# Two-operand GpSimd work of the mixers moved to VectorE, ScalarE and TensorE in five places, and the ranges of a group norm taken one by one

## The chip, the cores and the metric

One core of a Trainium2 chip runs the whole kernel. The metric is the device time of one execution in microseconds (us), the median of three runs. The engines are TensorE (PE in the profile, its weight loads PEld), VectorE (DVE), ScalarE (ACT), GpSimd (POOL) and SyncE (SP), which issues most transfers.

## The reference, cut to what matters

One decoder layer over 512 tokens and 16 meta tokens, width 1024, in float32: a mixer with two kinds of heads, then a mixture of experts.

```python
xn = _rmsnorm(h, norm_mix_w)                      # h: 528 x 1024
r, k, v, qm, km, vm, om, gm = split(xn @ w_in)
y_a = _rwkv7_time_mix(xn, r, k, v, ...)           # 8 heads of 64
y_b = _mlstm_mix(qm, km, vm, om, gm, ...)         # 4 heads, chunks of 64 in the reference
h = h + concatenate([y_a, y_b]) @ w_out
h = h + _hmoe(_rmsnorm(h, norm_ffn_w), ...)       # top group of 4, then 2 of its 8 experts
return _rmsnorm(h, norm_final_w)[:, 16:]

# in _rwkv7_time_mix
a = sigmoid(a0 + (xa @ a_la) @ a_lb)
kk = normalized(k * k_k);  k = k * (1 + (a - 1) * k_a)
S = S * decay + (S @ -kk) * (kk * a) + v * k      # a step for each token
y = group_norm(S @ r) * lnx_w + lnx_b
y = (y + sum(r * k * r_k) * v) * g
```

## The kernel before, in words

The tokens lie along the columns of tiles of 128 channels x 528 tokens. The recurrence is computed in chunks of 64 tokens (and one of the 16 meta tokens), which takes the inverse of a unit triangular matrix for each chunk and head.

**Head (lines 546 to 701).** The eight blocks of the input arrive as tiles xT[k]. For each, ScalarE makes the scaled high part and VectorE the low part (`xl`, a scalar-tensor-tensor), and TensorE multiplies them with the first two blocks of the input projection. `squares` (L613) squares each block, on ScalarE for even k and on VectorE for odd k, and GpSimd adds each square to `acc` (L620). Then two ones-matmuls with `acc` (L695) and Ln and Exp give `rstd`. `lora_mix` and `lora_split` (L647, L656) on VectorE and ScalarE prepare the LoRA block, the first projection of the planned part.

**The planned part (from L642 to `W.run()`).** The mixers are generators, each with a rank (`W.add`). A planner, `Weave` (L355), runs the one of lowest rank that is ready. What "ready" means is told by `Clock` (L181), a written table of costs for each engine; GpSimd's tensor_tensor has a rate of its own there, twice VectorE's. The order in which generators issue instructions is the program's order for TensorE and SyncE, which are under a manual schedule; the other engines' instructions are ordered by the tile scheduler.

- `projections` (L1008): the blocks of the input projection in the order of `PLAN`, each 48 matmuls (24 for "o"). `prepare` (L671) makes the high part of the next block on ScalarE, and its low part, 128x1024, on `lo_by`: GpSimd once mark "P3" is set (the products of all four head pairs are done), VectorE before that, and VectorE again when the recurrence is over, but for kind "q".
- `decays`, `norms`, `heads`, `products` (L778 to 957): for each of four pairs of heads j, the decay, the normalized key and the blocks MV, Bbd and Kbd that the products on TensorE read. In `heads` (L836) GpSimd does the diagonal of MV, nk times alpha, kp times kx, two of the four copies into E, and r times r_k times kp, in two instructions.
- `inverse0` and `inverse` (L1357, L1372): `interleaved` (L1335) inverts by column steps of two dependent tensor_tensor instructions, a product and an addition; the 16-row inverse runs on GpSimd, the 32-row one on VectorE. Matmuls on 32x32 blocks finish the latter.
- `chain` (L1476): the recurrence over nine chunks. At its end it takes the tiles `Gw` and `sq` and sets the mark "chain".
- `variances`, `variance`, `outputs_a`, `gated` (L1545 to 1584): the group norm of each of four ranges of 128 tokens (Square, a matmul, Ln), one Exp over all four ranges, and then for each range the product with the gate (on GpSimd), two VectorE instructions and the split into high and low parts, `ya`.
- `states` (L1191), `gates`, `scores`, `outputs_b`: the mLSTM heads. `mixer`: the output projection, the residual, the router. `prefetch` fetches expert weights as soon as there is room.

Memory is handed out by `Space` and `Arena`: `A.get` takes a tile at once or fails, `W.room` lets the generator wait until there is room.

**Experts (from L2053).** Sixteen pairs of experts, twelve weight blocks of 1 MiB each. A block is fetched when a buffer is free.

Of the kernel before, what the change touches and what calls it, by code (L numbers as in the profile page):

```python
# [17 lines left out]
L = 528  # L18
# [417 lines left out]
def layer(ctx, tc, a, out, dbg=None, stop=None):  # L436
# [145 lines left out]
    acc = A.get([128, L], name="acc")  # L582
# [29 lines left out]
    A.put(idle_)  # L612
    def squares(k):  # L613
        sq = A.get([128, L], name="sq") if k else acc
        if k % 2:
            V.tensor_tensor(sq, xT[:, k], xT[:, k], op=OP.mult)
        else:
            S.activation(sq, xT[:, k], AF.Square)
        if k:
            G.tensor_tensor(acc, acc, sq, op=OP.add)  # L620
            A.put(sq)

    first_block(0, 2)
    for k in range(8):
        S.activation(xh[k], xT[:, k], AF.Copy, scale=c("nmw", k))
        V.scalar_tensor_tensor(xl[k], xT[:, k], c("nmw", k), xh[k].bitcast(F32), op0=OP.mult, op1=OP.subtract)
        proj_k(pk, kh_, kl_, k)
        if not k:
            first_block(2, 8)
            A.put(kraw)  # L630
        if k == 2:
            k1h, k1l, kput1 = split_block(stream.loaded.pop(0), hi_by=S, lo_by=V)
            for i in range(k):
                proj_k(pk1, k1h, k1l, i)
        if k >= 2:
            proj_k(pk1, k1h, k1l, k)
            squares(k - 2)
    for k in range(6, 8):
        squares(k)

# [30 lines left out]
    def prepare(kind):  # L671

        lo_by = V if late() and kind != "q" or "P3" not in W.marks else G
# [19 lines left out]
    pss = B.get(2, "pss", rest)  # L693
    for h in range(2):
        P.matmul(pss[:, h, :264], m("ones"), acc[:, 264 * h:264 * h + 264], start=True, stop=True)  # L695
# [4 lines left out]
    A.put(xT, acc)  # L700
# [135 lines left out]
    def heads():  # L836

        for j in range(4):
# [5 lines left out]
            G.tensor_tensor(MV[:, :, 128:192], i64[:, None].to_broadcast([128, 8, 64]),  # L844
                            DT[:, j, 1:9][:, :, None].to_broadcast([128, 8, 64]), op=OP.mult)
            G.tensor_scalar(mv0[:, NM:], i64, DT[:, j, 0:1], 0.0, op0=OP.mult, op1=OP.add)
            G.tensor_tensor(nk, nk, al, op=OP.mult)
            kp = al
            S.activation(kp, al, AF.Identity, scale=c("k_a", j), bias=dv[:, 12 + j:13 + j])
            G.tensor_tensor(kp, kp, kx[j], op=OP.mult)  # L850
# [13 lines left out]
            for p in range(2):  # L864
                for i in range(2):
                    (S.copy if p else gcopy)(E[i][PAR[p], :, j, p], MV[PAR[p], 4 * i:4 * i + 4, 0:128])
            G.tensor_scalar(r[:, NM:], r[:, NM:], c("r_k", j), 0.0, op0=OP.mult, op1=OP.add)
            G.tensor_tensor(r[:, NM:], r[:, NM:], kp[:, NM:], op=OP.mult)
# [322 lines left out]
    def states():  # L1191
# [3 lines left out]
        for tb in range(-1, 3):  # L1195
# [6 lines left out]
            kw = A.get([128, 4, 64], name="kw")  # L1202
# [154 lines left out]
    def inverse0():  # L1357
# [8 lines left out]
        yield from interleaved(G, XL0, lambda s: NL0[:, s + 1:, s], NM, tm0, 99)  # L1366
# [5 lines left out]
    def inverse():  # L1372
# [39 lines left out]
        A.put(NL, XL, Y1, Y2, *tmps, *Zs)  # L1412
        dump("X", Bt)
# [62 lines left out]
    def chain():  # L1476
# [40 lines left out]
        Gw = A.get([128, 4, T], name="Gw")  # L1517
        sqs.append(A.get([128, 4, 4, 128], name="sq"))
        B.put(pU, pY)
        every.extend(rest)  # L1520
# [24 lines left out]
    def variances():  # L1545

        f = "p j x -> p (j x)"
        yield from until("chain")
        for tb in range(4):
            W.add(1, variance(tb, yT[tb].rearrange(f), sqs[0][:, tb].rearrange(f)))  # L1550
        yield from until(*(f"var{tb}" for tb in range(4)))
        S.activation(sqs[0], sqs[0], AF.Exp, scale=-0.5)
        W.mark("var")
# [13 lines left out]
    def outputs_a():  # L1567
        yield from until("var", "Gw")
        for tb in range(4):
            ya[tb] = yield from W.room(A, 2, [128, 4, 128], F32R, "ya", (ar_s[tb],))  # L1570
            gated(tb, sqs[0][:, tb])
            W.mark(f"ya{tb}")
            yield
        A.put(sqs[0], BV, Gw)

    def gated(tb, sq):
        y = yT[tb]
        G.tensor_tensor(y, y, Gw[:, :, 128 * tb:128 * tb + 128], op=OP.mult)
# [748 lines left out]
```

## Time and profile before

| | |
|---|---|
| median of 3 runs | 916.93 us (914.76 to 918.5) |
| the profiled execution | 914.68 us |
| its span, first to last instruction | 912.8 us |
| PE busy | 841.9 us (92%) |
| DVE busy | 434.1 us (48%) |
| ACT busy | 270.8 us (30%) |
| POOL busy | 224.0 us (25%) |
| mean granted TensorE clock | 0.96 |

The span is what the profile shows; the time of the execution has some two microseconds around it. Most instructions of the mixers carry the line L304, that of a helper that records every operation, so they are told apart by engine, operation, tile and shape: arF is the arena of most tiles, arS and arR those of high and low parts, arW that of the output weights, accs the accumulators of TensorE. A busy PE is one with a matmul in flight, and the clock is the share of full speed that was granted to it. What a stage's busy time means depends on what it waits for, so the rows below are taken by stage.

### The profile page before, as it was taken

What the parts mean: (1) busy time and instruction counts of PE and PEld (TensorE: products, weight loads), DVE (VectorE), ACT (ScalarE), POOL (GpSimd) and SP (SyncE); (2) the same over time, 40 slices, a digit from 0 to 9 for tenths busy, and PEclk for the clock granted to TensorE, in tenths of its full rate; (3) what the DMA queues carried; (4) which work ended last, traced back from release to release, by engine and by line L of the source; (5) the groups of instructions that cost most, each with busy time, mean ns of one, the idle gap of its engine ahead of it and who ended that gap; (6) DMA issues with size and microseconds to landing.
All of it is one profiled execution on the core that took longest, in us unless ns stands there. A gap on an engine that the chain in (4) does not pass through costs nothing.

```text
span 912.8 us, 13508 instructions
## 1 busy us (share of the span) xinstructions
PE 841.9 (92%) x5385; PEld 517.7 (57%) x5386; DVE 434.1 (48%) x821; ACT 270.8 (30%) x522; POOL 224.0 (25%) x297
## 2 busy tenths in 40 slices
PE   7969989879999997998999999999999999989994
PEld 5868878769999776887343444433344323323331
DVE  7677766995444668328132333423333223313324
ACT  5756655324435773333100110101110011001102
POOL 6064553553545156254000000000000000000002
PEclk9989999986998999998999999999999999999998
DMA  6200113201100137928999999999999999999992
GB/s 236 70 24 24 47 70 83 65 27 55 47 25 25 48 107 291 405 78 332 394 419 421 420 421 419 421 420 420 421 418 420 422 421 421 420 420 422 420 379 96
DMA packets 45141, 239.50 MB, mean 262 GB/s; under 512 B 8944, under 2 KB 9328, under 8 KB 21008
## 3 DMA queue, kind: packets, MB, share of 16 engines
q1 hardware_dynamic: 42192, 228.56, 62.5%
q0 software_dynamic: 2160, 7.87, 2.2%
q10 hardware_dynamic: 720, 2.15, 0.6%
q8 instruction: 44, 0.72, 0.3%
q14 instruction: 25, 0.20, 0.1%
HBM read 234.36 MB, written 4.19 MB: 261 GB/s over the span
## 4 chain that ended last, share of the span: by engine, by line
PE 55%; DMA 20%; DVE 15%; ACT 5%; issue 3%; POOL 2%; SPq 0%; ACTq 0%; DVEq 0%; POOLq 0%
PE accs L304 22%; PE accs L2067 17%; DVE arF L304 10%; PE accs L2112 7%; DMA arF<-wgu 7%; ACT arF L304 3%; PE accs L1990 3%; DMA arH<-wgu 2%; DMA arF<-wdn 2%; DMA arN<-wdn 2%; DMA arN<-wgu 2%; DMA arM<-wgu 2%; PE accs L1991 2%; DMA arF<-wo 1%; POOL arF L304 1%
## 5 line engine op out<-in xcount | busy, mean ns | idle before, releaser
L304 PE MATMUL accs<-arS,arR 128*128 128x264 f32 (+2 forms) x1136 | 182.6, 312 | 10.6 <-DVE arR L304 5.0
L304 PEld LDWEIGHTS accs<-arS,arR 128*128 128x128 f32 (+1 forms) x1136 | 160.4, 198 | 23.1 <-DVE arR L304 5.4
L304 PE MATMUL accs<-arF 64*64 64x64 f32 (+18 forms) x1223 | 129.7, 271 | 29.1 <-DVE arF L304 15.6
L1993 DVE TENSOR_TENSOR arF<-arF,accs 128x512 f32<-128x512 f32 x124 | 80.8, 684 | 102.5 <-PE accs L1991 101.0
L304 PEld LDWEIGHTS accs<-arF 128*128 128x128 f32 (+7 forms) x1202 | 103.5, 159 | 41.3 <-DVE arF L304 11.6
L2067 PE MATMUL accs<-arF 128*64 128x512 f32 x488 | 115.8, 605 | 5.9 <-DMA arF<-wgu 5.9
L1803 POOL DMA_INDIRECT arM<-hd,arF x15 | 14.3, 956 | 380.0 <-DVE arF L1794 368.6
L304 POOL TENSOR_TENSOR arF<-arF 128x528 f32<-128x528 f32 (+13 forms) x101 | 90.7, 901 | 65.9 <-DVE arF L304 44.0
L304 DVE TENSOR_TENSOR arF<-arF 64x16 f32<-64x16 f32 (+33 forms) x183 | 90.5, 541 | 6.5 <-POOL arF L304 4.2
L2089 ACT ACTIVATE arF<-accs,arF 128x512 f32<-128x512 f32 x16 | 11.0, 687 | 252.4 <-PE accs L2067 252.4
L2067 PEld LDWEIGHTS accs<-arF 128*64 128x64 f32 x488 | 32.3, 138 | 76.0 <-issue 57.4
L304 ACT ACTIVATE arF<-arF 128x528 f32<-128x528 f32 (+8 forms) x108 | 57.9, 559 | 49.6 <-DVE arF L304 34.1
L2122 DVE SCALAR_TENSOR_TENSOR arO<-accs,arF,arO 128x1024 fp32r<-128x1024 f32 x15 | 19.3, 1284 | 103.8 <-ACT arO L2121 103.8
L304 POOL TENSOR_SCALAR arF<-arF 64x256 f32<-64x256 f32 (+9 forms) x97 | 55.4, 573 | 44.0 <-ACT arF L304 19.3
L2112 PE MATMUL accs<-arF 128*64 128x512 f32 x280 | 62.5, 595 | 0.5 <-issue 0.5
L304 ACT COPY arF<-accs 64x256 f32<-64x256 f32 (+6 forms) x119 | 43.2, 370 | 65.4 <-PE accs L304 31.2
L1990 PE MATMUL accs<-arO,OHT 128*128 128x512 f32 x124 | 57.4, 463 | 0.0
L304 DVE TENSOR_TENSOR arF<-accs,arF 128x528 f32<-128x528 f32 (+7 forms) x81 | 35.5, 462 | 34.5 <-PE accs L304 20.8
L2067 PE MATMUL accs<-arN,arF 128*64 128x512 f32 x200 | 47.5, 600 | 2.6 <-DMA arN<-wgu 2.5
L1991 PE MATMUL accs<-arO,OHT 128*128 128x512 f32 x124 | 48.9, 394 | 0.0
L2067 PE MATMUL accs<-arM,arF 128*64 128x512 f32 x200 | 46.9, 600 | 1.7 <-DMA arM<-wgu 1.7
L304 PE MATMUL accs<-arW,arS 128*128 128x512 f32 x192 | 47.7, 406 | 0.0
(140 smaller groups left out, 924.2 us busy)
## 6 DMA issues: line engine op xcount, KB each, us to landing
arF<-wgu SPq DMA_DIRECT2D x61, 1024.0 KB, 19.8
arF<-wdn SPq DMA_DIRECT2D x35, 1024.0 KB, 20.4
arN<-wgu SPq DMA_DIRECT2D x25, 1024.0 KB, 19.8
arM<-wgu SPq DMA_DIRECT2D x25, 1024.0 KB, 19.8
arH<-wgu SPq DMA_DIRECT2D x16, 1024.0 KB, 20.9
arN<-wdn SPq DMA_DIRECT2D x15, 1024.0 KB, 21.1
arF<-wb SPq DMA_DIRECT2D x23, 512.0 KB, 3.6
arH<-wdn SPq DMA_DIRECT2D x5, 1024.0 KB, 20.0
```

The lines of the kernel that those rows point to most:

```text
L304: r = f(*args, **kw)
L1803: nc.gpsimd.indirect_dma_start(out=xt[p % 2], out_offset=None, in_=hd, in_offset=bass.IndirectOffsetOnAxis(ap=idx[:, p % 2:p % 2 + 1], axi ...
L1990: P.matmul(pq, lhs, oh[:, hs], start=True, stop=False)
L1991: P.matmul(pq, lhs, ol[:, hs], start=False, stop=True)
L1993: V.tensor_tensor(hv, hv, pq, op=OP.add)
L2067: P.matmul(pgu[64 * e:64 * e + 64, h], x[:, k, 64 * e:64 * e + 64], w[:, D * e + 512 * h:D * e + 512 * h + 512], start=(k == 0), stop=(k = ...
L2089: S.activation(av, pgu[:, 0], AF.Silu, scale=r1_)
L2112: P.matmul(pdn[64 * e:64 * e + 64, h], aT[:, k, 64 * e:64 * e + 64], w[:, D * h + 512 * e:D * h + 512 * e + 512], start=(k == 0), stop=(k ...
L2122: V.scalar_tensor_tensor(ol, pdf, g1_, oh.bitcast(F32), op0=OP.mult, op1=OP.subtract)
```

## The change

Seven edits:

1. `squares`: every block is squared on ScalarE; VectorE adds the squares in pairs (odd k), and the ones-matmuls sum the four pairs in PSUM (`summed`), two of them inside the head's loop, two where the sum was formed before. `acc` and its seven GpSimd additions go.
2. `prepare`: the low parts stay on VectorE until a new mark, "inverse", which `inverse` sets at its end, instead of "P3".
3. `heads`: the diagonal of MV, nk times alpha and kp times kx go to VectorE; all four copies into E are ScalarE's; r times r_k times kp is one scalar-tensor-tensor on VectorE.
4. `inverse0`: the 16-row inverse's steps run on VectorE.
5. `chain`, `variances`: `sq` is four tiles of 128x512 instead of one of 128x2048, with an Exp for each; `Gw` and these tiles are taken with `W.room`.
6. `gated`: the product with the gate goes to VectorE.
7. `states`: `kw` is taken with `W.room`.

```diff
+    pss = B.get(2, "pss", rest)
+    sqs2 = []
+
     def squares(k):
-        sq = A.get([128, L], name="sq") if k else acc
+        sqs2.append(A.get([128, L], name="sq"))
+        S.activation(sqs2[k], xT[:, k], AF.Square)
         if k % 2:
-            V.tensor_tensor(sq, xT[:, k], xT[:, k], op=OP.mult)
-        else:
-            S.activation(sq, xT[:, k], AF.Square)
-        if k:
-            G.tensor_tensor(acc, acc, sq, op=OP.add)
-            A.put(sq)
+            V.tensor_tensor(sqs2[k], sqs2[k], sqs2[k - 1], op=OP.add)
+
+    def summed(k):
+
+        for h in range(2):
+            P.matmul(pss[:, h, :264], m("ones"), sqs2[k][:, 264 * h:264 * h + 264], start=(k == 1), stop=(k == 7))
...
         if k >= 2:
             proj_k(pk1, k1h, k1l, k)
-            squares(k - 2)
-    for k in range(6, 8):
         squares(k)
+        if k == 5:
+            summed(1)
+        if k == 7:
+            summed(3)
...
-        lo_by = V if late() and kind != "q" or "P3" not in W.marks else G
+        lo_by = V if late() and kind != "q" or "inverse" not in W.marks else G
...
-    pss = B.get(2, "pss", rest)
-    for h in range(2):
-        P.matmul(pss[:, h, :264], m("ones"), acc[:, 264 * h:264 * h + 264], start=True, stop=True)
+    summed(5)
+    summed(7)
...
-            G.tensor_tensor(MV[:, :, 128:192], i64[:, None].to_broadcast([128, 8, 64]),
+            V.tensor_tensor(MV[:, :, 128:192], i64[:, None].to_broadcast([128, 8, 64]),
...
-            G.tensor_tensor(nk, nk, al, op=OP.mult)
+            V.tensor_tensor(nk, nk, al, op=OP.mult)
...
-            G.tensor_tensor(kp, kp, kx[j], op=OP.mult)
+            V.tensor_tensor(kp, kp, kx[j], op=OP.mult)
...
-                    (S.copy if p else gcopy)(E[i][PAR[p], :, j, p], MV[PAR[p], 4 * i:4 * i + 4, 0:128])
-            G.tensor_scalar(r[:, NM:], r[:, NM:], c("r_k", j), 0.0, op0=OP.mult, op1=OP.add)
-            G.tensor_tensor(r[:, NM:], r[:, NM:], kp[:, NM:], op=OP.mult)
+                    S.copy(E[i][PAR[p], :, j, p], MV[PAR[p], 4 * i:4 * i + 4, 0:128])
+            V.scalar_tensor_tensor(r[:, NM:], r[:, NM:], c("r_k", j), kp[:, NM:], op0=OP.mult, op1=OP.mult)
...
-            kw = A.get([128, 4, 64], name="kw")
+            kw, = yield from W.room(A, 1, [128, 4, 64], F32, "kw")
...
-        yield from interleaved(G, XL0, lambda s: NL0[:, s + 1:, s], NM, tm0, 99)
+        yield from interleaved(V, XL0, lambda s: NL0[:, s + 1:, s], NM, tm0, 99)
...
         A.put(NL, XL, Y1, Y2, *tmps, *Zs)
+        W.mark("inverse")
...
-        Gw = A.get([128, 4, T], name="Gw")
-        sqs.append(A.get([128, 4, 4, 128], name="sq"))
         B.put(pU, pY)
+        Gw, = yield from W.room(A, 1, [128, 4, T], F32, "Gw")
+        sqs.extend((yield from W.room(A, 4, [128, 4, 128], F32, "sq")))
...
-        S.activation(sqs[0], sqs[0], AF.Exp, scale=-0.5)
+        for sq in sqs:
+            S.activation(sq, sq, AF.Exp, scale=-0.5)
...
-        G.tensor_tensor(y, y, Gw[:, :, 128 * tb:128 * tb + 128], op=OP.mult)
+        V.tensor_tensor(y, y, Gw[:, :, 128 * tb:128 * tb + 128], op=OP.mult)
```

## Rows read from the trace of the kernel before

**Rows 1.** The page: busy share of the DMA engines in 40 slices, in tenths

```profile
DMA  6200113201100137928999999999999999999992
```

**Rows 2.** Chain of work that ended last: start us, us, what

```profile
216.45 82.21 PE accs L304 x1071
```

**Rows 3.** Busy us by stage: stage, length, engines (count), PEclk, DMA share, GB/s

```profile
57.00:65.00 8.00, 1.90 (x16) 1.68 (x14) 5.55 (x4) 3.90 (x7) 7.92 (x12) 0.77 0.00 0
65.00:77.00 12.00, 10.99 (x58) 9.98 (x59) 9.39 (x16) 4.72 (x12) 5.57 (x14) 0.87 0.17 46
...
164.00:208.00 44.00, 35.47 (x252) 33.25 (x252) 43.42 (x116) 15.36 (x35) 26.44 (x45) 0.88 0.13 37
...
216.00:300.00 84.00, 83.55 (x1079) 77.26 (x1080) 39.41 (x72) 33.40 (x66) 36.02 (x52) 0.88 0.11 33
```

**Rows 4.** The same view in steps of 5 us, one step

```profile
390.00:395.00 5.00, 5.00 (x18) 4.00 (x17) 0.00 (x0) 0.00 (x0) 0.00 (x0) 0.75 0.00 0
```

**Rows 5.** Groups by shape, DVE, 5 to 26.5 us: busy us, mean ns | idle

```profile
L304 DVE SCALAR_TENSOR_TENSOR arS<-arF,arS 128x528 fp32r<-128x528 f32 x8 | 10.3, 1318 | 0.5 <-ACT arS L304 0.5
L304 DVE TENSOR_TENSOR arF<-arF 128x528 f32<-128x528 f32 x4 | 6.2, 1546 | 1.0 <-DMA arF<-xT 1.0
```

**Rows 6.** Groups by shape, DVE, 29 to 50 us

```profile
L304 DVE TENSOR_TENSOR arQ<-arF,arR 128x1024 fp32r<-128x1024 f32 x3 | 3.7, 1221 | 0.2 <-ACT arR L304 0.2
...
L304 DVE SCALAR_TENSOR_TENSOR arF<-arF 128x528 f32<-128x528 f32 x2 | 1.5, 770 | 3.6 <-ACT arF L304 3.6
```

**Rows 7.** Groups by shape, POOL, 5 to 26.5 us

```profile
L304 POOL TENSOR_TENSOR arF<-arF 128x528 f32<-128x528 f32 x7 | 12.3, 1753 | 6.5 <-ACT arS L304 4.5 <-ACT arF L304 1.0 <-DVE arF L304 0.7
```

**Rows 8.** Timeline, end of the head: start us, us, what [idle before <-releaser]

```profile
24.26 2.54 DVE L304 TENSOR_TENSOR arF<-arF 128x512 f32<-128x512 f32 x3
...
26.84 1.04 ACT L304 CAST arQ<-arF 128x1024 fp32r<-128x1024 f32 x1 [8.16 <-DVE arF L304]
...
25.73 1.05 PE L304 MATMUL accs<-arF 128*128 128x264 f32 x4
27.93 0.76 PE L304 MATMUL accs<-arS,arQ 128*128 128x264 f32 x4 [1.15 <-ACT arQ L304]
```

**Rows 9.** Timeline of DVE and of PE, first pair of heads (j=0)

```profile
59.42 7.16 DVE L304 TENSOR_TENSOR arF<-arF 64x512 f32<-64x512 f32 x8 [2.83 <-POOL arF L304]
...
65.16 4.33 PE L304 MATMUL accs<-arF 128*128 128x192 f32 x16 [6.26 <-POOL arF L304]
```

**Rows 10.** Timeline of DVE and of PE, second pair of heads

```profile
94.26 2.12 DVE L304 TENSOR_TENSOR arQ<-arF,arR 128x1024 fp32r<-128x1024 f32 x1 [1.66 <-ACT arR L304]
...
98.52 0.76 PE L304 MATMUL accs<-arF 128*128 128x192 f32 x3 [1.12 <-ACT arF L304]
```

**Rows 11.** Groups by shape, DVE, 164 to 208 us, the inverse's steps

```profile
L304 DVE TENSOR_TENSOR arF<-arF 128x128 f32<-128x128 f32 x4 | 3.4, 909 | 0.0
L304 DVE TENSOR_TENSOR arF<-arF 128x126 f32<-128x126 f32 x10 | 3.2, 370 | 0.1
...
L304 DVE TENSOR_TENSOR arF<-arF 128x30 f32<-128x30 f32 x4 | 0.5, 187 | 0.0
```

**Rows 12.** Timeline of POOL, DVE and PE, gating

```profile
334.77 8.21 POOL L304 TENSOR_TENSOR arF<-arF 128x512 f32<-128x512 f32 x5 [0.58 <-ACT arF L304]
...
341.74 3.48 DVE L304 TENSOR_TENSOR arF<-arF 128x512 f32<-128x512 f32 x2
...
352.01 1.22 PE L304 MATMUL accs<-arS,arR 128*128 128x512 f32 x2 [5.01 <-DVE arR L304]
```

**Rows 13.** Timeline of ACT, before the group norm's Exp

```profile
317.94 1.28 ACT L304 ACT_TABLE_LOAD   x1
```

**Rows 14.** Timeline: ACT, recurrence's end and last numerator; PE, output projection

```profile
303.49 0.76 ACT L304 COPY arF<-accs 64x256 f32<-64x256 f32 x2
...
332.64 0.19 ACT L304 ACTIVATION_READ_ACCUMULATOR arF<-accs 128x1 f32 x1
...
360.23 2.10 PE L304 MATMUL accs<-arW,arS 128*128 128x512 f32 x8
```

More of the change, by code (lines that the diff above doesn't have):

```diff
@@ L579, in layer @@
         G.memset(t, 0.0)
-    acc = A.get([128, L], name="acc")
     kh_, kl_ = kput = [A.get([128, 1024], F32R, n) for n in ("whi", "wlo")]
@@ L699, in layer @@
     B.put(pss)
-    A.put(xT, acc)
+    A.put(xT, *sqs2)
     dump("rstd", rstd)
@@ L1549, in variances @@
         for tb in range(4):
-            W.add(1, variance(tb, yT[tb].rearrange(f), sqs[0][:, tb].rearrange(f)))
+            W.add(1, variance(tb, yT[tb].rearrange(f), sqs[tb].rearrange(f)))
         yield from until(*(f"var{tb}" for tb in range(4)))
-        S.activation(sqs[0], sqs[0], AF.Exp, scale=-0.5)
+        for sq in sqs:
+            S.activation(sq, sq, AF.Exp, scale=-0.5)
         W.mark("var")
@@ L1570, in outputs_a @@
             ya[tb] = yield from W.room(A, 2, [128, 4, 128], F32R, "ya", (ar_s[tb],))
-            gated(tb, sqs[0][:, tb])
+            gated(tb, sqs[tb])
             W.mark(f"ya{tb}")
             yield
-        A.put(sqs[0], BV, Gw)
+        A.put(*sqs, BV, Gw)
     def gated(tb, sq):
         y = yT[tb]
-        G.tensor_tensor(y, y, Gw[:, :, 128 * tb:128 * tb + 128], op=OP.mult)
+        V.tensor_tensor(y, y, Gw[:, :, 128 * tb:128 * tb + 128], op=OP.mult)
         V.tensor_tensor(y, y, sq, op=OP.mult)
```

## The prediction

> **What bounds the kernel now.** The page comes first: its line of DMA digits has a first 9 in the seventeenth slice of 40, falls to 2, and stands at 9 from the twentieth to the last but one [rows 1]. So there are two parts: the mixers, some 19 slices of 22.8 us or 434 us, in which transfers are sparse, and the experts, in which weights stream without a pause. In the chain of work that ended last TensorE leads the mixers, as in the one piece of 82.21 us from 216.45 [rows 2]. Before the second part the stream once stands still: nothing is moved from 390 to 395 us [rows 4]. All blocks for which there is room have been fetched by then, and the next ones wait for buffers that the end of the mixers frees. I read this so: whatever ends the mixers X earlier restarts the stream X earlier, its length is fixed, and the end moves by X.
>
> Inside the mixers I went to the table of stages [rows 3]. TensorE does 83.55 of the 84 us from 216 to 300, so there what was gained before is kept. It does only 1.90 of the 8 us from 57 to 65, and 35.47 of 44 us from 164 to 208, where VectorE is busy for 43.42: that stage, the 32-row inverse, is VectorE's. Next come groups by shape. VectorE's 128x528 scalar-tensor-tensor takes 1318 ns on the mean in the first 26.5 us, its tensor-tensor of that size 1546 ns [rows 5]; from 29 to 50 us, where GpSimd has almost nothing, the first takes 770 [rows 6]. In the slow stretch GpSimd runs seven adds of 1753 ns each [rows 7]. So a two-operand instruction of GpSimd makes VectorE wait. It is no transfer's doing: from 57 to 65 us none runs, GpSimd is busy for 7.92 of the 8 us [rows 3], and eight VectorE instructions of at most 64x512 need 7.16 us from 59.42 on [rows 9].
>
> The sum is made against the profiled execution: 914.68 us with a span of 912.8, 2.25 under the median 916.93 of the three runs. I take the same saving off the median.
>
> **1. Squares (head).** Out go seven GpSimd adds [rows 7]. In come four VectorE adds for four VectorE squares, four more squares on ScalarE, and six more ones-matmuls: four records, one pair of halves, cost 1.05 us [rows 8], so three further pairs cost 3.15. VectorE has eight scalar-tensor-tensors and four tensor-tensors there. Those eight lose 8 x (1318 - 770) = 4.4 us, the four lose 4 x (1546 - 770) = 3.1, with the former's clean time as the bound for the latter: 7.5 us together [rows 5, 6]. The last of them leads to the LoRA mix at 24.26 (2.54 us), the split, and TensorE's first matmul of that projection at 27.93 after a wait for ScalarE [rows 8]. ScalarE's four squares are dearer than nothing, but its line is idle most of that stretch: its wait before the cast is 8.16 us [rows 8]. Of the 3.15 us of ones-matmuls two pairs lie beside the waits of the head, about one in front of the projection. If all 3.15 are exposed I get 7.5 - 3.15 = 4.3; if none, 7.5. ScalarE as new pace of the head would take some of either. I take 5.5, nearer the lower end. Bounds: 3 to 7.5.
>
> **2. Heads.** For each of four j, VectorE gets four instructions that were GpSimd's (the diagonal, nk times alpha, kp times kx, and one scalar-tensor-tensor for the r_k pair); ScalarE gets two E copies. The price is four clean ones, at most 4 x 0.77 = 3.1 us per j on VectorE [rows 6]; for j above 0 TensorE runs projections meanwhile, and that cover must hold: without it up to 3 x 3.1 us come back. For j=0 nothing covers: TensorE stands 6.26 us until 65.16, behind a GpSimd chain [rows 9]. VectorE itself idles for the 2.83 us before 59.42 [rows 9], so from 56.6 on. In that idle time it can now do the diagonal and nk, then what stands before the first product (both halves of Bbd, one of B0bd): five steps of at most 0.77 end at 60.4. That saves 65.16 - 60.4 = 4.8 (4 if parts of Kbd slip between, at most 6.3, the whole wait). After that wait the clock fell: 0.77 granted in 57 to 65 and 0.87 in 65 to 77 [rows 3], so of the latter 12 us 12 x 0.13 = 1.5 us of TensorE's work were lost at the lower of the two levels, 1.2 instead of 2.4 GHz. A wait of 1.12 us at j=1 [rows 10] shows what is left then; I count the 1.5 as saved (0 to 1.5). At j=1 the split at 94.26 takes 2.12 us where a clean one takes 1.22 [rows 6, 10], and TensorE waits 1.12 behind it: 0.9. Sum 4.8 + 1.5 + 0.9 = 7.2.
>
> **3. Inverse.** Four low parts (1024 columns) leave GpSimd inside the stage; a fifth lies right behind. Each made one VectorE instruction hang: the 128x128 group has a mean of 909 over four, the undisturbed-by-splits 128x126 group 370 [rows 11], so one hang costs 4 x (909 - 370) = 2.16 us and four 8.6. On VectorE they cost 4 x 1.22 = 4.9 [rows 6]. The small inverse's 15 steps of two dependent instructions now come to VectorE too. At 187 ns, the mean of 128x30 [rows 11], thirty cost 5.6; at 370, as under contention, 11.1; overlapped in pairs perhaps 3.9. GpSimd's own small steps no longer slow VectorE, worth 0 to 3; I take 1.5. Net: -8.6 + 4.9 + 5.6 - 1.5 = +0.4 us (from -2.8 to +7.4). Who waits behind: casts of values and norms in VectorE's line, and through them TensorE.
>
> **4. Gating.** Four multiplies of y by the gate leave GpSimd, whose five in a row take 8.21 us; VectorE's pair beside them takes 3.48, 1.74 each [rows 12]. GpSimd keeps four others there (the o gate and the odd splits). So VectorE gains perhaps four stalls of 1 us and takes four clean multiplies of some 0.7. TensorE waits 5.01 us for VectorE's split [rows 12]. I take 1.0 saved (0 to 5).
>
> **5. Group norm, by ranges.** One Exp becomes four of a quarter of its width. A table load of 1.28 us stands between the last Ln and it [rows 13]. If the scheduler puts an Exp between two Ln, each crossing pays another, at most six: 7.7 us of ScalarE. I take nothing, since TensorE goes on with other work until the wait of 5.01 at 352.01 [rows 12]; the bound is 0 to 3. The Trainium skill ("ScalarE: Activation LUTs", Table sets) says that Ln then Exp need a single load, since one set has both; by it no order could cost more and that bound would be nothing, but here the load is there.
>
> The room waited for by kw is costed at nothing: the tile is small, and before it was had at once; what a wait costs stands under D.
>
> Sum: 5.5 + 7.2 - 0.4 + 1.0 = 13.3. Profiled 901.4, median **903.6 us**. No rows show the planner's new TensorE order; I put it at nothing, since TensorE stays full from 216 on, and at 5 us either way in the range.
>
> **Rivals.** A: the sum, 0.51.
> B, more is released: the small steps overlap (2.8 instead of -0.4: 3.2 more), the wait of 5.01 closes (4 more), and another clock fall goes, 1.5: 13.3 + 8.7 = 22, 895 us. For it: every stage has that pattern. Against: VectorE has more to do. Chance 0.19.
> C, the two engines take turns: what moves still queues, now on VectorE. The head keeps 4.3, j=0 only 2.4 (half of 4.8), the inverse pays its upper 7.4 and gating nothing: 0.7 lost, 917.6 us; with half of it in force (13.3 - 0.7) / 2 = 6.3 saved, 910.6. For it: VectorE is full in the inverse [rows 3]. Against: its own price for an instruction is less than half of GpSimd's [rows 6, 7]. Chance 0.16. The Trainium skill ("Perfetto Trace Analysis", Optimizing Scalar/DVE Operations) warns that offloading between the two might not help, as they share a read port; by that sentence C would be the rule.
> D, the room for Gw and the four range tiles: both are now waited for. Place: the end of the recurrence, 303.49. The next large release is that of the q/k tiles, after the last read at 332.64: 29 us later [rows 14]. The first output matmul at 360.23 hangs on this chain [rows 14], with nothing to put in front, so 903.6 + 29 = 933 us. It decides once the wait exceeds 18 us (921.5 - 903.6). Against: before, both were had there without a wait. Chance 0.09.
> E, the change does not do what it says: VectorE's long times are not GpSimd's doing. Then the head gains nothing, j=0 gains 2.4, the inverse pays 4.9 + 5.6: +8, 925 us. The stretch at 59.42 speaks against it [rows 9]. Chance 0.05.
>
> **Numbers.** This kernel's measurement can tell about 0.5% from no change, 4.6 us: faster is below 912.3, slower above 921.5. Faster: A 0.50, B 0.19, C 0.11 = 0.80. Same: A 0.01, C 0.05, D 0.02, E 0.01 = 0.09. Slower: D 0.07, E 0.04 = 0.11. The range takes A with its bounds, B, and C's better half: 889 to 914; D, E and C's rest are the two in ten left out.
>
> **What would show it.** Right: VectorE's 128x528 group near 770 ns in the head, the first LoRA matmul near 22.5; TensorE's wait at 58.9 under 2 us and the clock not falling behind it; no 1024-column GpSimd multiply or subtract from 164 to 208, and VectorE's stage about as long as now; the stop in the weight stream and its resumption some 13 us earlier. Wrong: a VectorE group still at 1.3 us in the head (E), an inverse longer by over 5 us (C), a hole after the recurrence (D), or a shift in the mixers that the stream does not follow.

## The result and the profile after

The changed kernel took 921.28 us (median of 20 runs), the kernel before 916.39 us (20 runs): ratio 1.0056 with a 95% interval of 1.0041 to 1.0072, so 0.56% or about 5 us **slower**. Forecast were 903.6 us and a range of 889 to 914. The profiled execution has a span of 919.6 us against 912.8.

VectorE's instructions became as short as forecast. Its groups by shape, 5 to 26.5 us, of the changed kernel (busy us, mean ns):

```profile
L304 DVE SCALAR_TENSOR_TENSOR arS<-arF,arS 128x528 fp32r<-128x528 f32 x8 | 6.2, 789 | 0.6 <-ACT arS L304 0.6
L304 DVE TENSOR_TENSOR arF<-arF 128x528 f32<-128x528 f32 x4 | 2.9, 723 | 0.0
```

In [rows 5] the same groups took 1318 and 1546 ns (the four of the second are squares there and sums of squares here). The stages of [rows 3], and one more stretch, 70 to 84 us, in the same columns:

```profile
57.00:65.00 8.00, 6.99 (x51) 6.81 (x50) 7.19 (x15) 5.40 (x10) 3.15 (x9) 1.00 0.22 68
65.00:77.00 12.00, 9.03 (x37) 6.67 (x36) 10.32 (x20) 6.11 (x15) 4.29 (x7) 0.72 0.15 44
164.00:208.00 44.00, 41.33 (x324) 39.50 (x323) 43.19 (x155) 19.24 (x45) 4.85 (x7) 0.98 0.22 65
216.00:300.00 84.00, 79.78 (x1112) 72.15 (x1110) 45.33 (x86) 35.64 (x78) 31.91 (x57) 0.88 0.08 23
...
70.00:84.00 14.00, 13.23 (x45) 10.63 (x46) 8.22 (x18) 8.68 (x17) 2.21 (x6) 0.51 0.00 1
```

The empty stage from 57 to 65 us is filled: TensorE works 6.99 of its 8 us instead of 1.90. But the next one is worse than before (clock 0.72), and the clock stands at 0.51, the lower of its two levels, from 70 to 84 us. From 216 to 300 us TensorE, full before, lacks 4.2 us. TensorE's timeline after (start us, us, what [idle before]):

```profile
24.82 2.43 PE L304 MATMUL accs<-arS,arQ 128*128 128x264 f32 x17
...
47.32 0.51 PE L304 MATMUL accs<-arR 64*128 64x264 f32 x2 [2.79 <-ACT arR L304]
...
59.28 2.84 PE L304 MATMUL accs<-arF 128*128 128x192 f32 x16 [1.01 <-DVE arF L304]
...
70.77 2.05 PE L304 MATMUL accs<-arF 128*128 128x80 f32 x5 [2.97 <-ACT arF L304]
...
203.81 9.43 PE L304 MATMUL accs<-arS,arR 128*128 128x264 f32 x76
213.17 2.03 PE L304 MATMUL accs<-arF 32*32 32x32 f32 x37
...
237.17 0.84 PE L304 MATMUL accs<-arF 64*16 64x64 f32 x16 [0.95 <-ACT arF L304]
```

The first LoRA matmul comes 3.1 us earlier than in [rows 8], the products of j=0 5.9 us earlier than in [rows 9], after 1.01 us of waiting instead of 6.26. Two waits for ScalarE are new, though: 2.79 us ahead of 47.32 and 2.97 us ahead of 70.77. The granted clock is at 0.50 from 49.8 to 56.6 us, where it was at 1.00 before, and at 0.51 from 70 to 84. And at 203.81 us 76 projection matmuls stand in front of the inverse's first 32x32 product, whose input was ready at about 207. Milestones of the profiled executions (us, from their timelines: starts, and for the recurrence the end of its last product; the inverse starts with VectorE's first transpose; e1 to e18 are the experiments below):

| kernel | first LoRA | products j=0 | inverse | first 32x32 | recurrence's end | first w_out | span |
|---|---|---|---|---|---|---|---|
| before | 27.93 | 65.16 | 158.9 | 209.0 | 302.5 | 360.2 | 912.8 |
| after | 24.82 | 59.28 | 159.8 | 213.2 | 306.4 | 365.1 | 919.6 |
| e1 | 28.33 | 62.15 | 158.8 | 208.3 | 300.6 | 356.5 | 908.0 |
| e7 | 23.76 | 55.84 | 153.1 | 200.9 | 291.0 | 348.4 | 901.9 |
| e5 | 25.00 | 60.74 | 156.9 | 205.6 | 296.7 | 358.7 | 911.3 |
| e18 | 26.05 | 61.78 | 159.6 | 207.5 | 298.6 | 351.2 | 903.9 |

All 5.9 us are gone when the inverse starts, its first product is 4.2 us late, and the end follows the mixers (+4.9 at w_out, +6.8 in the span).

Each row is a single execution. The kernels before, e12, e13 and e17 have the same order of TensorE and the same engines up to the recurrence's end, yet start the inverse at 158.9, 160.9, 161.4 and 158.6 us; after, e5, e16 and e18, alike up to the inverse, start it at 159.8, 156.9, 161.4 and 159.6. A difference of up to 4.5 us between two rows ahead of the inverse therefore says nothing by itself; a difference in length of one stretch that returns in several kernels does.

### The profile page after: what moved, and what is told of

Same layout as the page of the kernel before. It is cut to its first block, busy times and chain, and to the rows that moved or that the text cites. A ratio compares the mean times of both kernels' runs of the same rounds, so it can differ in the third digit from the quotient of the medians.

```text
span 919.6 us, 13512 instructions
## 1 busy us (share of the span) xinstructions
PE 852.1 (93%) x5397; PEld 527.3 (57%) x5398; DVE 427.5 (46%) x879; ACT 284.4 (31%) x541; POOL 151.7 (16%) x220
## 5 line engine op out<-in xcount | busy, mean ns | idle before, releaser
L304 PE MATMUL accs<-arS,arR 128*128 128x264 f32 (+2 forms) x1136 | 179.5, 309 | 4.9 <-DVE arR L304 2.5
L304 PE MATMUL accs<-arF 32*32 32x32 f32 (+18 forms) x1235 | 136.0, 279 | 26.0 <-DVE arF L304 15.6
L304 PEld LDWEIGHTS accs<-arF 128*128 128x128 f32 (+8 forms) x1214 | 108.4, 164 | 38.5 <-issue 13.1
L2072 PE MATMUL accs<-arF 128*64 128x512 f32 x440 | 102.9, 600 | 5.1 <-DMA arF<-wgu 5.1
L304 DVE TENSOR_TENSOR arF<-arF 128x512 f32<-128x512 f32 (+32 forms) x229 | 81.6, 409 | 6.5 <-DMA arF<-wr 5.1
L304 ACT ACTIVATE arF<-arF 128x528 f32<-128x528 f32 (+6 forms) x115 | 61.1, 552 | 50.7 <-DVE arF L304 27.4
L2117 PE MATMUL accs<-arF 128*64 128x512 f32 x320 | 71.4, 596 | 1.2 <-ACT arF L2103 0.7
L2072 PEld LDWEIGHTS accs<-arF 128*64 128x64 f32 x440 | 28.5, 136 | 67.1 <-issue 47.8
L304 POOL TENSOR_TENSOR arF<-arF 64x256 f32<-64x256 f32 (+7 forms) x44 | 40.8, 927 | 103.0 <-DVE arF L304 76.8
L1995 PE MATMUL accs<-arO,OHT 128*128 128x512 f32 x124 | 57.4, 463 | 0.0
L2117 PEld LDWEIGHTS accs<-arF 128*64 128x64 f32 x320 | 22.2, 136 | 45.1 <-issue 33.1
```

The source lines that it names most:

```text
L304: r = f(*args, **kw)
L1995: P.matmul(pq, lhs, oh[:, hs], start=True, stop=False)
L2072: P.matmul(pgu[64 * e:64 * e + 64, h], x[:, k, 64 * e:64 * e + 64], w[:, D * e + 512 * h:D * e + 512 * h + 512], start=(k == 0), stop=(k = ...
L2117: P.matmul(pdn[64 * e:64 * e + 64, h], aT[:, k, 64 * e:64 * e + 64], w[:, D * h + 512 * e:D * h + 512 * e + 512], start=(k == 0), stop=(k ...
```

## The experiments

Runs are named e1 to e18 in the order in which they were made. Every kernel is timed against the kernel before on the same chip, and the brackets behind a ratio are its 95% interval. A gain in us is the ratio's distance from 1 (or from another ratio) times 916.4; the interval of a difference of two ratios is put together from theirs as the root of the sum of squares.

### Engines or order: e1, e2

The planner books each instruction, that is, enters it with its price into the account of an engine, and derives TensorE's order from these accounts. One wrapper lets an instruction run on one engine and be booked on another:

```diff
+    VG, SG = Told(nc.vector, "G", clock), Told(nc.scalar, "G", clock)
-            G.tensor_tensor(nk, nk, al, op=OP.mult)
+            VG.tensor_tensor(nk, nk, al, op=OP.mult)
...
-        yield from interleaved(G, XL0, lambda s: NL0[:, s + 1:, s], NM, tm0, 99)
+        yield from interleaved(VG, XL0, lambda s: NL0[:, s + 1:, s], NM, tm0, 99)
```

e1 does so with all moves but the squares; e2 is the mirror image (changed kernel, moved work on `nc.gpsimd`, booked on VectorE).

> All moves of the change from GpSimd to VectorE and ScalarE except the squares of the head (heads of the mixers, low parts, the inverse of the first rows, gating), but the planner's cost table is told that GpSimd still does them, so that TensorE's and SyncE's instructions stand in exactly the order of the kernel before. Theory P (the engines gain what was forecast, and the new order of TensorE that the planner derives from the moved costs gives it away): the wait ahead of the products of j=0 (6.26 us before) falls under 2 us, nothing downstream is worse, and the time is 905 to 911 against about 916.4. Rival E (VectorE's added work is itself the loss, whatever the order): 918 to 923, with the first 32x32 matmuls of the inverse late as in the changed kernel. Rival F (a stretch further on is the limit, so neither engines nor order matter much): 915 to 918.

Measured: 908.03 us, ratio 0.9920 (0.9894 to 0.9947).

> The mirror image: the changed kernel with its TensorE order, its head, its rooms and ranges, but the moved work of the heads, low parts, first-row inverse and gating is done by GpSimd again, while the planner is told that VectorE and ScalarE do it. Theory P: slower than both kernels, 924 to 932 against about 921 after and 916.4 before: the waits of the kernel before on top of an order that was made without them. Rival E: about 911 to 916, since the load that hurt is off VectorE and the head's gain of about 5 us stays. Rival F: 915 to 918.

Measured: 932.83 us, ratio 1.0193 (1.0168 to 1.0219).

The engines' moves save 7.3 us in the old order; the rest of the change (the new order, the ranges, the waits for buffers, and the whole of the new head) costs 17.7 us when the moved work is back on GpSimd, just over the 932 that theory P gave. Rival E falls, and theory P's split into a gain of the engines and a loss of the rest holds. But in e1 the inverse starts at 158.8 us, as before: part of the gain is lost early, which theory P did not say.

### Single parts, re-planned: e3, e4

```diff
-            G.tensor_tensor(acc, acc, sq, op=OP.add)
+            V.tensor_tensor(sqs2[k], sqs2[k], sqs2[k - 1], op=OP.add)
...
+            P.matmul(pss[:, h, :264], m("ones"), sqs2[k][:, 264 * h:264 * h + 264], start=(k == 1), stop=(k == 7))
```

> The kernel before with the head's part alone (squares all on ScalarE, pairs summed on VectorE, the rest summed by the ones matmuls). The forecast's own term was 5.5 us less, 911. Theory P: the first LoRA matmul comes about 3 us earlier as in the changed kernel (24.8 against 27.9), and what arrives at the end differs from that by whatever the re-planned order does: 910 to 919. Rival E: 3 us less, 913, since the head alone adds little to VectorE.

Measured: 916.23 us, ratio 1.0011 (0.9993 to 1.0029).

e4 is the heads' hunk of the change:

```diff
-            G.tensor_tensor(kp, kp, kx[j], op=OP.mult)
+            V.tensor_tensor(kp, kp, kx[j], op=OP.mult)
```

> The kernel before with the mixers' heads alone moved to VectorE and ScalarE, planner told so. The forecast's own term was 7.2 us less, 909. Theory P: the products of j=0 start 4 to 6 us earlier, but the re-planned order puts new waits and half-clock stretches of TensorE behind them, and the end is 912 to 920; less time than this with the order kept is what the run with the old order shows. Rival E: 917 to 922, as the added VectorE work of the heads delays the copies that free the product banks.

Measured: 914.91 us, ratio 0.9997 (0.9980 to 1.0014).

Neither part alone is a gain clear of noise once the planner has drawn its consequences.

### One term at a time, order kept: e9, e10, e11, e13

Only the squares (odd ones on ScalarE, adds on VectorE), the heads, the inverse with the low parts, or the gating; booked as before. In the traces of all the runs with the order kept, TensorE's matmuls stand in the order of the kernel before, by tiles and shapes.

```diff
-            G.tensor_tensor(acc, acc, sq, op=OP.add)
+            VG.tensor_tensor(acc, acc, sq, op=OP.add)
```

> One term alone, order kept: only the head's squares leave GpSimd (odd squares on ScalarE, adds on VectorE), planner told as before. The forecast gave the head 5.5 us (bounds 3 to 7.5); with all other moves already made the same edit was worth 4.9 us (908.0 to 903.2). If the term stands by itself, 909 to 912. If it only pays together with the heads' move (because the next wait, 6.26 us ahead of the products of j=0, takes it back), 914 to 916.

Measured: 912.25 us, ratio 0.9957 (0.9936 to 0.9977).

> One term alone, order kept: only the mixers' heads move to VectorE and ScalarE, planner told that GpSimd does them. The forecast's term was 7.2 us less (4.8 for the wait ahead of j=0, 1.5 for the clock behind it, 0.9 at j=1). In the run with all moves but the squares the wait ahead of j=0 was gone, but the inverse started where it did before (158.8 us). If the half-clock stretches behind new short waits take the gain back, 913 to 916, and the inverse starts at 157 to 160 us. If the forecast's term stands, 907 to 910.

Measured: 914.14 us, ratio 0.9979 (0.9959 to 0.9998).

> One term alone, order kept: only the first rows' inverse and the low parts of the weights in that stretch move to VectorE, planner told that GpSimd does them. The forecast's term was 0.4 us more (bounds 2.8 less to 7.4 more), since thirty small VectorE operations replace the waits behind GpSimd's 1024-column ones. If that balance is right, 914 to 917 and the inverse lasts as long as before (48.5 us from first transpose to the third batch of transposes). If most of the 7.5 us of the run with all moves came from here, 909 to 912.

Measured: 916.05 us, ratio 1.0003 (0.9982 to 1.0024).

> One term alone, order kept, ranges and buffers as before: only the four products of the gating move to VectorE. The forecast's term was 1.0 us less (0 to 5): the 5.01 us wait of TensorE at 347 us in the kernel before shrinks. If the rest of the joint gain is the gating by itself, 909 to 911; if the term stands, 913 to 916, and the rest lies in the moves' paying only together.

Measured: 910.60 us, ratio 0.9953 (0.9928 to 0.9978).

The squares' term stands (3.9 us), the heads' does not (1.9 of 7.2), the inverse is nothing, and the gating gives 4.3. In e13, VectorE's two multiplies beside the gating and TensorE's waits behind it:

```profile
340.32 1.28 DVE L304 TENSOR_TENSOR arF<-arF 128x512 f32<-128x512 f32 x2
```

```profile
348.19 5.37 PE L304 MATMUL accs<-arS,arR 128*128 128x512 f32 x22 [1.24 <-DVE arR L304]
...
356.55 0.66 PE L304 MATMUL accs<-arF 128*128 128x128 f32 x4 [1.67 <-ACT arF L304]
```

A pair takes 1.28 us where it took 3.48, and 1.24 and 1.67 us of waiting stand for the 5.01 of [rows 12].

### Terms together, order kept: e14, e15, e7

> Two terms together, order kept: squares and heads. The sum of the two single runs is 5.8 us less, 910. If they pay more together (the heads' shorter wait is no longer followed by half-clock stretches at 50 to 60 us), 905 to 908 and the inverse starts at 152 to 155 us. If less, 912 to 914.

Measured: 910.78 us, ratio 0.9943 (0.9918 to 0.9967).

> Squares, heads and inverse, order kept; against the run with the gating too (903.2) it shows what the gating adds, against the run with squares and heads what the inverse adds. If each term stands by itself, 0 to 1 us from the run with squares and heads and 1 to 3 us above 903.2, so 904 to 907. If the gating holds the rest, 907 to 909.

Measured: 904.36 us, ratio 0.9869 (0.9831 to 0.9906).

> The run with the old order, and the seven adds of the head's squares taken from GpSimd too (odd squares on ScalarE, adds on VectorE, planner told as before). If VectorE's long times in the head are GpSimd's doing, its 128x528 operations there fall from about 1.3 us to near 0.77 us and the first LoRA matmul comes 1 to 3 us earlier. Theory G (gains ahead of the inverse are paid back by TensorE's half-clock stretches): the inverse still starts at 157 to 160 us and the time is 906.5 to 909. Rival (gains ahead of the inverse last): 903 to 906.

Measured: 903.17 us, ratio 0.9859 (0.9829 to 0.9888). It is e1 with the squares: 12.9 us less than before, the fastest kernel of the study, in TensorE's old order behind the head. My theory G was wrong here: the inverse starts at 153.1 us, so what the squares gain does last. Terms do not add: the inverse, nothing alone, is worth 6.8 us (2.7 to 10.9) on top of squares and heads (its own stretch, up to the first 32x32 product, falls from 50.6 us in e14 to 47.6 in e15, which shows 3 of them). The gating gives 0.9 us on top of the rest where it gave 4.3 alone, but the 0.9 have an interval from -3.5 to 5.3, so that difference is not shown.

### What the shorter waits do to the clock: e8

From 40 to 160 us, the kernels before, e10 and e1, and after (columns of [rows 3]):

```profile
40.00:160.00 120.00, 103.86 (x716) 96.23 (x714) 83.56 (x120) 72.68 (x136) 58.40 (x90) 0.96 0.17 50
```

```profile
40.00:160.00 120.00, 106.72 (x723) 98.74 (x722) 86.54 (x142) 78.95 (x146) 35.04 (x62) 0.95 0.19 55
```

```profile
40.00:160.00 120.00, 109.67 (x718) 101.36 (x716) 84.41 (x136) 78.13 (x144) 33.58 (x62) 0.91 0.18 51
```

```profile
40.00:160.00 120.00, 105.86 (x673) 97.01 (x672) 82.25 (x134) 73.91 (x140) 33.49 (x62) 0.89 0.17 47
```

In e10 TensorE waits 2.9 us less than before, in e1 5.8 us less (109.67 busy against 103.86), and the clock falls from 0.96 to 0.95 and to 0.91: in e1 120 x 0.05 = 6 us. In the 120 us e1 gets through as many matmuls as before, 718 for 716. These are single executions: e12 and e13, alike with the kernel before up to there, show 0.94, so e10's 0.95 says nothing, and e8, close to e1, has 0.93. Nor does the loss hold for the whole: over six executions e1's mean clock is 0.960, that of the kernel before beside it 0.958. Before, part of the lower level lay on idle time, 57 to 65 us [rows 3]; in e1 the falls lie on work. One follows waits of 1.2 and 1.3 us at 72 and 75 us, where VectorE's new instructions stand between the copies that free banks. So e8 gave two of them back to GpSimd:

```diff
-            VG.tensor_tensor(MV[:, :, 128:192], i64[:, None].to_broadcast([128, 8, 64]),
+            G.tensor_tensor(MV[:, :, 128:192], i64[:, None].to_broadcast([128, 8, 64]),
```

> The run with the old order, but in the mixers' heads two operations that nobody waits for soon (the product with the diagonal, and r times r_k times k') stay on GpSimd as in the kernel before. In the run with the old order VectorE does both (about 0.7 us each) between the copies that free the banks of the LoRA matmuls, which wait 1.2 and 1.3 us at 72 and 75 us, and TensorE's granted clock is 0.50 after. Theory Q (these in-order VectorE operations make those waits, and the clock falls behind them): the waits at 72 to 76 and 103 to 107 us shrink under 0.7 us, the half-clock stretches behind them go, the inverse starts 3 to 6 us earlier, and the time is 903 to 907. Rival R (GpSimd's two operations delay VectorE by as much as they relieve it): the inverse starts as late as before, 907 to 911.

Measured: 908.32 us, ratio 0.9926 (0.9900 to 0.9951), level with e1. TensorE's waits are still there. The second block below shows VectorE ahead of them: in e1 an instruction of its own and a moved one behind it, in e8 the same instruction of its own:

```profile
73.27 0.99 PE L304 MATMUL accs<-arR 64*128 64x264 f32 x6 [1.27 <-ACT arF L304]
...
76.52 1.68 PE L304 MATMUL accs<-arR 64*128 64x264 f32 x6 [1.34 <-DVE arF L304]
```

```profile
70.41 0.69 DVE L304 SCALAR_TENSOR_TENSOR arF<-arF 128x512 f32<-128x512 f32 x1
71.02 0.68 DVE L304 TENSOR_TENSOR arF<-arF 128x512 f32<-128x512 f32 x1
...
70.72 1.38 DVE L304 SCALAR_TENSOR_TENSOR arF<-arF 128x512 f32<-128x512 f32 x1
```

Theory Q's gain does not come, and the trace shows why e8 cannot settle it: the 0.68 us that VectorE is spared it loses again, since its instruction at 70.72 takes 1.38 us while GpSimd does the returned product from 70.50 to 71.55. That is rival R. What makes the waits, and why the clock falls behind a wait of 1.3 us in one execution and not in another, stays open.

### Where the new order loses: e5, e6

e5 is the changed kernel, with only the first rows' inverse (`VG` as in e1) and the low parts of that stretch booked on GpSimd. e6 books all moves so.

```diff
-        lo_by = V if late() and kind != "q" or "inverse" not in W.marks else G
+        lo_by = V if late() and kind != "q" or "P3" not in W.marks else G if "inverse" in W.marks else VG
```

> The changed kernel with all its work on the changed engines; only the planner is told that GpSimd still does the inverse of the first rows and the low parts of the weights in the inverse's stretch. Theory I (what was lost sits at one place: told of more VectorE work, the planner takes the inverse to end later, puts two more projections ahead of its small matmuls, and the recurrence lacks them afterwards): the first 32x32 matmul comes within 1.5 us of the last transpose (6.5 us in the changed kernel), the gaps of TensorE between 230 and 310 us go, and the time is 909 to 914 against 921. Rival H (the order of the mixers' heads lost as much or more): 916 to 920, and the recurrence begins earlier without a better end. Rival N (the order as such means nothing and the run with the old order was quick for another reason): 919 to 922.

Measured: 915.40 us, ratio 1.0007 (0.9986 to 1.0029).

The projection matmuls (those that read the arena of weight halves) between the inverse's start and its first 32x32 product, and from there to the recurrence's end, in the kernels before, after and e5. Columns: stretch, length, TensorE's busy us (count), ...

```profile
158.90:209.00 50.10, 31.95 (x227) 30.19 (x225) 0.00 (x0) 5.25 (x5) 10.71 (x5) 0.90 0.15 43
209.00:302.50 93.50, 43.76 (x280) 38.37 (x279) 5.09 (x7) 6.71 (x9) 9.25 (x5) 0.87 0.12 37
```

```profile
159.80:213.20 53.40, 42.32 (x323) 40.28 (x322) 9.09 (x6) 6.58 (x7) 0.00 (x0) 0.97 0.24 73
213.20:306.40 93.20, 30.71 (x187) 25.83 (x186) 7.94 (x9) 6.40 (x9) 0.62 (x1) 0.87 0.09 24
```

```profile
156.90:205.60 48.70, 32.36 (x234) 30.47 (x232) 6.16 (x5) 5.24 (x5) 0.00 (x0) 0.92 0.15 47
205.60:296.70 91.10, 42.26 (x285) 37.14 (x285) 5.09 (x7) 6.71 (x9) 7.76 (x4) 0.89 0.13 40
```

After the change 96 more projection matmuls (two blocks) stand ahead of the inverse's product and 93 fewer behind it, where the recurrence's waits need them. Booked as before they are back in place, the first product follows the transpose at once, and the recurrence has no holes. The stretch up to the first product takes 53.4 us after the change and 48.7, 48.4 and 47.9 in e5, e16 and e18, the one behind it 93.2 against 91.1 in e5 and e18, so this is no accident of one execution. It is worth 0.49% or 4.5 us (2.1 to 6.9; ratios 1.0056 and 1.0007), a little less than theory I said: the time missed its 914. Behind the recurrence e5 loses again: 62.0 us from its end to the first w_out product, against 57.4 in e7 (table).

> The changed kernel with its head, rooms and ranges, all work on the changed engines, and the planner told that GpSimd does the heads' work, the low parts, the first rows' inverse and the gating. Theory I: close to the run above, 908 to 914, since the inverse's place in the order is the same in both. Rival H: clearly below the run above, 905 to 909. If the head's part is worth its 3 us further on, it ends 2 to 4 us below the 908.0 of the run with the old order; if the clock and the waits before the inverse eat it, it ends level with that run or above.

Measured: 925.74 us, ratio 1.0105 (1.0080 to 1.0131). None of the theories had this: e6 has yet another order of TensorE and is the slowest kernel with the changed engines. It also has the ranges, which e12 to e18 look at; its inverse starts at 163.3 us, 6.4 later than in e5. Why that order is so slow ahead of the inverse stays open.

### Behind the recurrence: e12, e16, e17, e18

e12 is the change's gating, ranges and waits for buffers in the kernel before. e16 is e5 without ranges and waits for buffers, gating booked as before. e17 and e18 are e12 and e5 with the ranges joined again, the waits kept:

```diff
-        sqs.extend((yield from W.room(A, 4, [128, 4, 128], F32, "sq")))
+        sqs.extend((yield from W.room(A, 1, [128, 4, 4, 128], F32, "sq")))
```

> The part behind the recurrence alone, as the change has it (gating on VectorE, ranges of the group norm one by one, buffers waited for), planner told the truth. The order of TensorE differs from before only there, in few places. The forecast's terms: 1.0 us less for the gating (0 to 5), nothing for the ranges (0 to 3 us more). If they stand, 913 to 916. If the ranges and the waits for buffers are what the changed kernel loses behind the recurrence, 917 to 920.

Measured: 917.48 us, ratio 1.0016 (0.9997 to 1.0034).

> The run with the inverse told as before (915.4: the changed kernel's head and heads, its order up to the recurrence), but behind the recurrence ranges and buffers as in the kernel before, gating on VectorE and told as before. If the waits for buffers and the ranges lose what that run lost behind the recurrence (its first w_out product came 62 us after the recurrence's end, 57 us in the run with the old order), 909 to 912. If they are free and the loss lies ahead of the inverse or in TensorE's order as such, 914 to 917.

Measured: 909.29 us, ratio 0.9925 (0.9900 to 0.9949).

> The part behind the recurrence as changed (gating on VectorE, planner told the truth, buffers waited for), but one tile and one Exp for the group norm as in the kernel before. Theory X (the four Exp fall between the Ln of the ranges, each crossing costs ScalarE a table load, and TensorE waits behind them): three table loads between 296 and 368 us instead of nine, TensorE's waits of 3.1 and 1.8 us at 306 and 329 us go, and the time is 909 to 912, as with the gating alone (910.6). Rival W (the waits for buffers cost it): 915 to 918, as with the ranges (917.5).

Measured: 911.72 us, ratio 0.9965 (0.9951 to 0.9980).

> The changed kernel with the inverse told as before (915.4), and one tile and one Exp for the group norm. Theory X: two or three table loads in that stretch instead of eight, the waits of 3.1 and 3.0 us at 301 and 310 us go, and the time is 908 to 911, as without ranges and waits for buffers (909.3). Rival W: 914 to 917.

Measured: 906.23 us, ratio 0.9899 (0.9876 to 0.9923).

The waits for buffers show no cost (e17 against e13; e18 against e16, which also differ in the booking of the gating). The ranges cost 1.0007 - 0.9899 = 1.08% or 9.9 us (7.0 to 12.8) in e5, more than theory X said, and 4.7 us (2.5 to 6.8) in e12. The changed kernel itself was not run without them. Its own profile has six table loads from 296 to 368 us, three more than the kernel before. ScalarE's table loads from 296 to 368 us, in before, e12 and e17 (count | busy us, mean ns):

```profile
L304 ACT ACT_TABLE_LOAD x3 | 3.8, 1283 | 0.1
```

```profile
L304 ACT ACT_TABLE_LOAD x9 | 11.5, 1283 | 0.2
```

```profile
L304 ACT ACT_TABLE_LOAD x3 | 3.8, 1283 | 0.1
```

ScalarE's and TensorE's timelines in e5 (the 128x512 from a bank is the Ln of a range, that from arF alone its Exp), and ScalarE's in e18:

```profile
308.41 0.63 ACT L304 ACTIVATE arF<-arF 128x512 f32<-128x512 f32 x1
...
310.72 1.28 ACT L304 ACT_TABLE_LOAD   x1
312.02 0.69 ACT L304 ACTIVATE arF<-accs,arF 128x512 f32<-128x512 f32 x1
312.73 1.28 ACT L304 ACT_TABLE_LOAD   x1
```

```profile
304.66 5.08 PE L304 MATMUL accs<-arF 128*128 128x512 f32 x30 [3.11 <-ACT arF L304]
312.76 5.22 PE L304 MATMUL accs<-arF 128*128 128x512 f32 x34 [3.02 <-ACT arF L304]
```

```profile
313.47 1.28 ACT L304 ACT_TABLE_LOAD   x1
314.76 1.91 ACT L304 ACTIVATE arF<-arF 128x2048 f32<-128x2048 f32 x1
```

Though the code writes the four Exp behind the last Ln, each now depends on its own range alone; they run between the four Ln, with a load at each crossing, and TensorE's wait of 3.02 us ends when the Ln of 312.02 is done. The other wait, 3.11 us, ends before the first load: so that one is not the loads' doing. Both are gone in e18 (one Exp, two loads, TensorE's longest wait from 280 to 370 us 0.97 us), and from the recurrence's end to the first w_out product e18 takes 52.6 us for e5's 62.0. How the 9.9 us divide between the loads and TensorE's order around the ranges stays open.

## Why the prediction was wrong

**The step that failed** is that two terms of the sum were put at nothing because TensorE was thought to have other work.

The larger is **the group norm's ranges** (step 5). The six extra loads were priced at up to 7.7 us of ScalarE and then put at nothing, "since TensorE goes on with other work until the wait of 5.01", with a bound of 3. The six extra loads came, nine for three in e12 and eight for two in e5 against e18, but TensorE did not have that other work: joining the ranges again is worth 4.7 us in the one and 9.9 in the other. The Trainium skill ("ScalarE: Activation LUTs", Table sets) lets a Ln and an Exp share one load; the trace of e5 has a load of 1.28 us between each Ln and Exp, so the measurement decides against it.

The other is **the planner's order**: "the planner's new TensorE order; I put it at nothing, since TensorE stays full from 216 on". TensorE was full there because the planner had kept projections for it; told of more VectorE work in the inverse, it spent two blocks of them ahead of the inverse's first product, and TensorE was not full any more. That alone is 4.5 us, still inside the 5 us that the range allowed for the order; with the ranges on top the time left the range.

What is left from e18 to e7 is 0.9899 to 0.9859 or 3.7 us (0.2 to 7.1). It is a net figure: e18 reaches the recurrence's end 7.6 us later than e7 (298.6 for 291.0) and the first w_out product only 2.8 us later. The order ahead of the inverse, with the new waits of some 3 us, and the head's extra ones-matmuls lie in the first part and were not told apart; what gives 4.8 us back behind the recurrence stays open. 4.5 + 9.9 + 3.7 = 18.1 us is the way from the changed kernel over e5 and e18 to e7; the shares could differ if the steps were taken in another order.

**Point by point.**
- Mechanism of the engines' part: right. VectorE's 128x528 group is at 789 ns, and e13's pair at 0.64 us each. Rival E is out. Rivals C and E, at 917.6 and 925 us, lie nearest to the result, but not by their mechanisms: in the old order the same moves save 12.9 us. The sentence of the Trainium skill ("Perfetto Trace Analysis", Optimizing Scalar/DVE Operations) that offloading between VectorE and GpSimd might not help doesn't hold for this direction here.
- The sum of the engine terms, 13.3, against 12.9 in e7 (10.3 to 15.7): right by luck, since errors cancel. Squares 5.5: 3.9 (2.1 to 5.9). Heads 7.2: 1.9 alone (0.2 to 3.8), and with the squares 5.2 (3.0 to 7.5) for a forecast of 12.7. The wait at j=0 went as forecast (the products start at 60.65 us in e10, for the 60.4 worked out), but the clock, counted as 1.5 us saved, fell further on; in e1's profile that took about 6 us. Inverse +0.4: 0.3 alone, 6.8 saved once squares and heads are moved. Gating 1.0: 4.3 alone, within its bounds of 0 to 5.
- Signs: the first LoRA matmul came at 24.82 for 22.5; e7, which has no extra ones-matmuls, has it at 23.76, so they explain at most half of the miss. The wait at 58.9 fell under 2 us, but the clock fell further on. No 1024-column two-operand GpSimd work is left from 164 to 208 us. The stop in the weight stream did not come 13 us earlier: from 390 to 395 us, where it stood before, 424 GB/s flow after the change; e7 has the stop earlier, from 380 to 385 (8 GB/s).
- Rival D: not seen. With the waits for buffers kept, e17 is within the interval of e13.
- The reading that whatever ends the mixers X earlier moves the end by X held within 2 us: e7's first w_out product is 11.9 us earlier than before, its span 10.9 us shorter; after the change it was 4.9 later and 6.8 longer.

## What to carry to other kernels

Where the order of one engine is derived from booked costs of the others, a moved instruction is two changes: it runs elsewhere, and it is booked elsewhere. Run it once with the old booking to see the first alone; here that version (903.2 us) beat both kernels. When one instruction becomes several, list what they may now fall between (here Exp between Ln), and ask which waits have no work left in front of them; and where a wait of TensorE is removed, check whether its granted clock holds in what follows.

## What the runs showed of the hardware

- Taking away waits did not raise TensorE's clock in the stretch behind them: with 5.8 us less idle time from 40 to 160 us e1's profile shows 0.91 for 0.96. From 65 to 76 us e1's longest wait of TensorE is 1.34 us and the clock is at 1.00; from 76.2 to 83.0 TensorE is busy throughout and the clock is at 0.50.
- The granted clock is not settled by the order of the instructions. It stood at the lower level for 14 us behind a wait of 2.97 us in the changed kernel, while in e5, whose order of TensorE is the same up to there, it was at the upper level from 72 to 78 us, right behind a wait of 3.10 us, and fell only from 78 to 82 (0.58). Kernels with the same order started the inverse between 156.9 and 161.4 us (e5, after, e18, e16).
- Over the 20 runs of the changed kernel the time goes from 913.2 us at a mean granted clock of 0.962 to 926.8 at 0.941. Over all executions the mean clock is 0.948 in e2 and 0.950 in e6 and the changed kernel, the three slowest, and 0.963 in e7, the fastest.
- In e5 a table load of 1.28 us stands between each Ln of the group norm and the Exp behind it, and again before the next Ln.
- With GpSimd's two-operand work gone, VectorE's instructions of 128x528 take 0.72 to 0.79 us where they took 1.32 to 1.55. One returned product of GpSimd was enough to make a 128x512 of VectorE take 1.38 us for 0.69 (e8, e1).
